# Emission order: products of generators that are due within a fixed time follow another generator's products at once

## The chip, the cores and the metric

One Trainium2 chip, one of its cores. The metric is the device time of one execution in microseconds (us), lower is better. The kernel before takes 3057.91 us (median of three runs, 3056.65 to 3059.26).

## What is computed

A two-layer backbone over 256 context and 256 latent tokens of width 2048. In each layer:

```python
xn  = rmsnorm(h) * (1 + scale) + shift           # shift, scale, gate = silu(c) @ ada_w + ada_b
u   = xn @ w_in                                  # one wide input projection
y_a = (groupnorm(wkv_scan(...)) + bonus) * silu(gate_a) @ w_out_a    # bidirectional RWKV-7, 16 heads of 64
y_b = (pool(u) @ pool_w) * silu(gate_b) @ w_out_b
h   = h + gate * ((mg0 * y_a + mg1 * y_b) @ w_out)                   # mg = sigmoid of columns of u
```

and a final rmsnorm of the latent half. The scan runs over 256 context tokens first and then over 256 latent tokens, in both directions.

## The kernel before, in words

All 512 tokens lie side by side in the free dimension; features lie on the 128 partitions. Weights stream from HBM in blocks of 512 KB into three buffers `wr`; each block is split on ScalarE into a high part `whi` and on VectorE into a low part `wlo`, and a projection of 128 outputs adds three products (high by high, high by low, low by high) for each of 16 slices of the input, 48 products of 512 (or, in layer 1, often 256) columns. These projections are the **main work**: a list of units, each of chunks and steps (`Main`, L366); one step is three products.

Beside it run **generators** (Python generators, L1371), in this order of precedence: `chain` (the scan over blocks of 64 tokens: tiles `ps_z`, `ps_a`, then `ps_y`, `ps_p`, `ps_y`), `gnorm` (`ps_c`, `ps_v`), `inv` (inverses of triangular blocks: `ps_M`, then `ps_Z` and `ps_W` in turn over six levels, `ps_R`, `ps_X`, `ps_T`, `ps_V`; one such generator in layer 0, two in layer 1), `prep` (`ps_kk`, `ps_d`, `ps_a`, `ps_b`, `ps_vr`) and `open_y`. A generator yields the time at which its next step is due. For a step with products that is `MG[l]` after its inputs are ready: 1000 ns in layer 0, 600 ns in layer 1.

The kernel is emitted in one pass with a clock for each engine (`E["pe"]`, `E["act"]`, ...; `clk`, L122), which are estimates in ns written into the kernel. `run` (L516) decides what comes next on all queues: if some generator's step is due (`t <= E["pe"]`), the first such one is emitted; otherwise `NS` = 2 steps of the main work (six products). Each engine executes its instructions in the order in which they were emitted.

The modulation vectors (`ada_blocks`, L559) are main work too. A block of `n` weight pieces adds its products into one tile `ps_ada`; after the last, `post` copies the sums to the one buffer `ada_r` (four small copies, ScalarE and VectorE in turn) and puts off the rest, `fin` (L595), to the time at which `ada_r` is expected: four products of `ada_r` with `comb` and some small VectorE operations. `flush_fins(n)` (L225) emits put-off `fin`s until no more than `n` are left. `step` calls `flush_fins(1)` (L466) before a unit's `pre`; `post` calls `flush_fins(0)` (L586) before it overwrites `ada_r`. Blocks of two pieces in succession stand in two places: in the first stretch of the kernel, interleaved with the units `ps_st`, and in the output projection of layer 0 (L1547), where each of the 16 units is a projection interleaved with one piece (`zipped`, L348): four steps of the projection (12 products), one of the piece, and so on, four times.

Of the kernel before, what the change touches and what calls it, by code (L numbers as in the profile page):

```python
# [8 lines left out]
R32 = mybir.dt.float32r  # L9
# [21 lines left out]
NU = (0, 1)  # L31
ZD = (0, 0)
N1, LA0, G0, LAG = 2, 20, 2, 4
AH, PACE, MG = 400.0, 600.0, (1000.0, 600.0)

V_MU, V_W0, V_A0, V_KK, V_KA, V_RK = 0, 24, 40, 56, 64, 80
# [10 lines left out]
def kernel(  # L47
# [65 lines left out]
    E = dict(pe=0.0, act=0.0, dve=0.0, pool=0.0, sp=0.0)  # L113
    rt, rd, old = {}, {}, {}

    def nm(ap):
        return ap.tensor.name

    def rdy(*aps):
        return max(rt.get(nm(a), 0.0) for a in aps)  # L120

    def clk(eng, cost, o, ins, lag=60.0):  # L122
        t = max(E[eng], rd.get(old.get(nm(o)), 0.0))
        for a in ins:
            t = max(t, rt.get(nm(a), 0.0))
        t += cost
        E[eng] = t
        rt[nm(o)] = t + lag
        for a in ins:
            rd[nm(a)] = t + lag  # L130
# [29 lines left out]
    def size(ap):  # L160
        n = 1
        for s in ap.shape[1:]:
            n *= s
        return n

    def mm(out, lhsT, rhs, start=True, stop=True, dep=True):
        nc.tensor.matmul(out=out, lhsT=lhsT, rhs=rhs, start=start, stop=stop)  # L167
        n, m = size(rhs), size(lhsT)
        dt = lhsT.dtype
        if dt == F32:  # L170
            c = 110 if m <= 32 else 360 if n < 32 else 1.6 * n if n > 64 else 190 if m > 64 else 78
        elif dt == R32:
            c = max(0.4225 * n, 109) + 75 * (kind[0] != dt)
        else:
            c = 28 if m > 64 else 18
        kind[0] = dt
        clk("pe", c, out, (lhsT, rhs) if dep else (), 200.0)

    kind = [R32]

    def act(out, in_, func=AF.Copy, scale=1.0, bias=None):
        kw = {} if bias is None else dict(bias=bias)
        nc.scalar.activation(out=out, in_=in_, func=func, scale=scale, **kw)  # L183
        c = (50 if psum(in_) else 90) + 0.84 * size(out) + 93 * ((not isinstance(scale, float)) + (bias is not None))
        clk("act", c, out, (in_,), 140.0)
# [4 lines left out]
    def tt(out, a, b, op, eng="dve"):  # L190
        ENG[eng].tensor_tensor(out=out, in0=a, in1=b, op=op)  # L191
        clk(eng, 65 + (1.05 if eng == "dve" else 2.0) * size(out), out, (a, b), 140.0)

    def stt(out, a, s, b, op0, op1):
        nc.vector.scalar_tensor_tensor(out=out, in0=a, scalar=s, in1=b, op0=op0, op1=op1)  # L195
        clk("dve", 65 + 1.05 * size(out), out, (a, b), 140.0)

    def ts(out, a, s1, op0, s2=None, op1=None, eng="dve"):
        kw = {} if op1 is None else dict(op1=op1)
        ENG[eng].tensor_scalar(out=out, in0=a, scalar1=s1, scalar2=s2, op0=op0, **kw)  # L200
        n = size(out)
        c = 75 + 1.8 * n if eng == "pool" else 120 + 0.95 * n if psum(a) else 60 + 0.52 * n if n > 300 else 75 + 0.65 * n
        clk(eng, c, out, (a,), 140.0)

    def cp(out, a, eng="dve"):
        ENG[eng].tensor_copy(out=out, in_=a)
        clk(eng, 50 + (0.7 if eng == "dve" else 3.8) * size(out), out, (a,), 140.0)
# [17 lines left out]
    def flush_fins(n):  # L225
        while len(fins) > n:
            late.remove(fins[0])
            fins[0][1]()

    def later(t, fn):  # L230

        x = (t, fn)
        late.append(x)
        return x

    def do_late(force=False):
        i = 0
        while i < len(late):
            if force or late[i][0] <= E["pe"]:
                late.pop(i)[1]()  # L240
            else:
                i += 1
# [239 lines left out]
    def pieces(src, load, ck, **kw):  # L482

        out = []
        for i in range(0, src.shape[1], load):
            g = dict(src=src[:, i:i + load], **kw)
            out += [dict(src=src[:, j:j + ck], grp=g, sl=slice(j - i, j - i + ck)) for j in range(i, i + load, ck)]
        return out
# [23 lines left out]
    def due(x):  # L512

        return max(x[0], piv.free("iv", x[1])) if isinstance(x, tuple) else x

    def run():  # L516

        while True:
            do_late()
            best, bt, held = None, None, True  # L520
            for g in gens:
                while g[1] is None:
                    g[1] = next(g[0], "end")
                    if g[1] is None:
                        break
                    held = False
                if g[1] == "end" or g[1] is None:
                    continue
                t = due(g[1])
                if best is None or t < bt:  # L530
                    best, bt = g, t
                if t <= E["pe"]:
                    best, bt = g, t
                    break
            gens[:] = [g for g in gens if g[1] != "end"]
            if best is None or bt > E["pe"]:
                mt = M.time()
                if mt is not None and (best is None or max(mt, E["pe"]) <= bt):
                    for _ in range(NS):
                        M.step()  # L540
                        do_late()
                        mt = M.time()
                        if mt is None or mt > E["pe"] + SL:
                            break
                    continue
            if best is None:
                if not gens and M.empty():
                    break
                if late:
                    do_late(True)  # L550
                elif held:
                    raise RuntimeError("stuck")
                continue
            E["pe"] = max(E["pe"], bt)
            best[1] = next(best[0], "end")
        do_late(True)


# [6 lines left out]
    def ada_block(l, b0, i, n, st, after, pre0, bank, slot):  # L565
        b = b0 + i
        nr = 2 * n

        def pre():
            if pre0:  # L570
                pre0()
            if i == 0:
                pl, tg = bank or (pmm, "mm")
                st["ps"] = pl.tile([128, T], F32, tag=tg, name="ps_ada")

        def mk(j):
            def step(c):
                for g in range(4):
                    mm(st["ps"][32 * g:32 * g + nr, 0:256], svp[:, 4 * j + g, 2 - 2 * i:2 - 2 * i + nr],
                       c["r"][:, g, :], start=i == 0 and j == 0, stop=i == n - 1 and j == 3)  # L580
            return (j, step)

        def post():
            if i < n - 1:
                return
            flush_fins(0)  # L586
            for g in range(4):
                q = slice(32 * g, 32 * g + nr)
                if g % 2:
                    cp(ada_r[q], st["ps"][q, 0:256])  # L590
                else:
                    act(ada_r[q], st["ps"][q, 0:256])
            fins.append(later(rdy(ada_r), fin))

        def fin():  # L595

            fins.pop(0)
            ps = st["ps"][:, 256:256 + 4 * n].rearrange("p (h i c) -> p h i c", h=2, c=2)
            for h in range(2):
                mm(ps[:, h].rearrange("p i c -> p (i c)"), ada_r[:, h * 128:(h + 1) * 128], comb[:, 0:2 * n])  # L600
            bias = lambda o, m: ve_t[:, l, o:o + m].unsqueeze(2).to_broadcast([128, m, 2])
            if b0 < KD:
                tt(modv[:, l, 0, b0:b0 + n, :], ps[:, 0], bias(V_AB + b0, n), ALU.add)
                m = modv[:, l, 1, b0:b0 + n, :]
                tt(m, ps[:, 1], bias(V_AB + 16 + b0, n), ALU.add)
                stt(m, m, 1.0, bias(V_NG + b0, n), ALU.add, ALU.mult)
            else:
                f = 2 * (b0 - KD)
                m = modv[:, l, 2, f:f + 2 * n, :]
                tt(m.rearrange("p (i h) c -> p h i c", h=2), ps,  # L610
                   bias(V_AB + 32 + f, 2 * n).rearrange("p (i h) c -> p h i c", h=2), ALU.add)
                ts(m, m, 0.5, ALU.mult)
            if after:
                for x in range(b0, b0 + n):
                    after(x)

        w = ada_w[l, b]
        if slot:
            ch = pieces(w, 8, 4, slot=slot)
        else:  # L620
            ch = pieces(w, 4, 4)
        return Unit(ch, [mk(j) for j in range(4)], pre, post, raw=True)


# [1062 lines left out]
```

## Time and profile before

| | before |
|---|---|
| median of three runs | 3057.91 us |
| the profiled execution | 3058.09 us |
| its span | 3056.3 us |
| TensorE busy (PE) | 2906.3 us, 95% |
| VectorE busy (DVE) | 1820.7 us, 60% |
| ScalarE busy (ACT) | 1457.3 us, 48% |
| GpSimd busy (POOL) | 149.7 us, 5% |
| mean granted TensorE clock | 0.978 |
| HBM | 139 GB/s over the span |

The span runs from the first to the last instruction. PE stands for matmul, PEld for the weight load that overlaps it, SP for the queue that issues DMAs. A matmul's end is modelled: successive matmuls overlap, so that the distance of their starts tells what one costs. By time the kernel falls into these stretches: until 160 us the first modulation vectors with the first projections (`ps_st`); 160 to 1381 us the projections of layer 0 with its generators; to 1597 us the two branch projections; to 1827 us the output projection of layer 0 with the modulation vectors of layer 1; to 1955 us the start of layer 1; to 2830 us its projections with its generators; then the rest.

### The profile page before, as it was taken

The numbers are of one execution on the slowest core, as the hardware profiler recorded it, in microseconds if no ns is written. First come the engines' busy times: TensorE is split into PE (matmuls) and PEld (weight loads), VectorE is DVE, ScalarE is ACT, GpSimd is POOL, SyncE is SP. The second block draws the span as 40 slices with busy tenths as digits, with TensorE's granted clock in tenths as the row PEclk, the third lists the DMA queues.
The fourth block names the chain that finished last, engine by engine and source line by source line (L and its number), as shares of the span: only waits on it lengthen the run. The fifth ranks groups of instructions, "written<-read, shape, count | busy, mean of one in ns | idle before, by whom it ended". The sixth has DMA issues, their size and how long they took to land.

```text
span 3056.3 us, 66262 instructions
## 1 busy us (share of the span) xinstructions
PE 2906.3 (95%) x27122; PEld 2292.5 (75%) x27122; DVE 1820.7 (60%) x4171; ACT 1457.3 (48%) x3092; POOL 149.7 (5%) x211
## 2 busy tenths in 40 slices
PE   5999999999999999998999989999999989999897
PEld 2687777767777777776876657887887768888797
DVE  3475666565655655534443235886786667775575
ACT  3254445445554554533222223666556646666454
POOL 2200000000000000000000002000000000000000
PEclk8999999999999999998999999999999989999899
DMA  9732222232333222327657764432333343344875
GB/s 361 256 121 72 78 76 91 72 116 94 112 111 118 87 80 87 94 88 248 205 190 225 234 222 124 141 117 85 108 94 111 119 127 99 111 122 129 260 251 161
DMA packets 158482, 427.74 MB, mean 140 GB/s; under 512 B 17376, under 2 KB 53600, under 8 KB 154080
## 3 DMA queue, kind: packets, MB, share of 16 engines
q1 hardware_dynamic: 133120, 390.32, 40.5%
q10 hardware_dynamic: 25056, 33.17, 3.0%
q8 instruction: 213, 3.49, 0.5%
q14 instruction: 93, 0.76, 0.1%
HBM read 389.21 MB, written 34.21 MB: 139 GB/s over the span
## 4 chain that ended last, share of the span: by engine, by line
PE 78%; DVE 8%; DMA 7%; ACT 5%; issue 2%; SPq 0%; POOL 0%; DVEq 0%; ACTq 0%; POOLq 0%
PE ps_mm L167 54%; PE ps_st L167 4%; DMA wr<-in_w_o 3%; DVE wlo L191 3%; PE ps_W L167 3%; PE ps_M L167 2%; PE ps_ada L167 2%; PE ps_y L167 2%; PE ps_a L167 2%; DMA wr<-in_w_in 2%; PE ps_Z L167 1%; PE ps_z L167 1%; PE ps_p L167 1%; ACT whi L183 1%; PE ps_T L1113 1%
## 5 line engine op out<-in xcount | busy, mean ns | idle before, releaser
L167 PE MATMUL ps_mm<-xh,whi 128*128 128x512 f32 (+1 forms) x2448 | 914.8, 374 | 8.2 <-ACT whi L183 3.1
L191 DVE TENSOR_TENSOR wlo<-wr,whi 128x512 fp32r<-128x512 f32 (+1 forms) x932 | 636.7, 696 | 444.8 <-ACT whi L183 439.1
L183 ACT ACTIVATE whi<-wr 128x512 fp32r<-128x512 f32 (+1 forms) x932 | 567.1, 619 | 671.3 <-PE ps_mm L167 336.7
L167 PE MATMUL ps_mm<-xh,wlo 128*128 128x512 f32 (+1 forms) x2448 | 855.2, 349 | 16.4 <-DVE wlo L191 15.7
L167 PE MATMUL ps_mm<-xl,whi 128*128 128x512 f32 (+1 forms) x2448 | 851.1, 348 | 0.0
L167 PEld LDWEIGHTS ps_mm<-xh,whi 128*128 128x128 f32 x2448 | 465.6, 190 | 91.9 <-issue 7.9
L167 PEld LDWEIGHTS ps_mm<-xh,wlo 128*128 128x128 f32 x2448 | 465.8, 190 | 83.5 <-DVE wlo L191 22.5
L167 PEld LDWEIGHTS ps_mm<-xl,whi 128*128 128x128 f32 x2448 | 467.6, 191 | 46.3 <-issue 1.0
L167 PE MATMUL ps_mm<-mgh,whi 128*128 128x512 f32 (+1 forms) x512 | 181.2, 354 | 2.9 <-ACT whi L183 2.9
L1024 DVE CAST_PREDICATED X<-pm_t,ps_W 128x128 f16<-128x128 uint8 x640 | 141.7, 288 | 65.2 <-PE ps_W L167 63.8
L167 PE MATMUL ps_mm<-mgh,wlo 128*128 128x512 f32 (+1 forms) x512 | 175.4, 343 | 0.0
L167 PE MATMUL ps_mm<-mgl,whi 128*128 128x512 f32 (+1 forms) x512 | 174.5, 341 | 0.0
L167 PE MATMUL ps_mm<-yh,whi 128*128 128x512 f32 (+1 forms) x512 | 129.0, 344 | 0.2 <-ACT whi L183 0.2
L167 PEld LDWEIGHTS ps_mm<-mgh,whi 128*128 128x128 f32 x512 | 98.2, 192 | 38.9 <-issue 19.3
L167 PE MATMUL ps_mm<-yl,whi 128*128 128x512 f32 (+1 forms) x512 | 125.4, 337 | 0.6 <-DVE m L195 0.5
L183 ACT ACTIVATE VS<-P 64x128 f32<-64x128 f32 x128 | 39.3, 307 | 167.3 <-DVE P L195 164.8
L183 ACT ACTIVATE zb<-ps_Z 128x512 f16<-128x512 f32 x144 | 85.2, 592 | 70.2 <-PE ps_Z L167 68.8
L167 PEld LDWEIGHTS <-X 64*64 64x64 f16 x2560 | 89.4, 110 | 35.7 <-issue 27.5
L191 POOL TENSOR_TENSOR nlo<-MM,n 64x512 f16<-64x512 f32 x48 | 62.8, 1308 | 1072.2 <-DVE X L1024 760.2
L167 PEld LDWEIGHTS ps_mm<-mgh,wlo 128*128 128x128 f32 x512 | 98.3, 192 | 14.5 <-DVE wlo L191 3.6
L167 PEld LDWEIGHTS ps_mm<-mgl,whi 128*128 128x128 f32 x512 | 98.4, 192 | 8.7
L167 PE MATMUL ps_ada<-wr,svp 128*4 128x256 f32 (+1 forms) x1024 | 83.2, 402 | 22.8 <-DMA wr<-in_ada_w 22.8
(258 smaller groups left out, 4353.2 us busy)
## 6 DMA issues: line engine op xcount, KB each, us to landing
wr<-in_w_in SPq DMA_DIRECT2D x306, 512.0 KB, 3.7
wr<-in_ada_w SPq DMA_DIRECT2D x128, 512.0 KB, 3.9
wbig<-in_ada_w SPq DMA_DIRECT2D x32, 1024.0 KB, 6.0
wr<-in_w_o SPq DMA_DIRECT2D x64, 512.0 KB, 4.8
wr<-in_w_b SPq DMA_DIRECT2D x32, 512.0 KB, 4.8
wr<-in_w_a SPq DMA_DIRECT2D x32, 512.0 KB, 4.0
wr<-in_w_st SPq DMA_DIRECT2D x32, 384.0 KB, 4.3
d_mg<-mth ACTq DMA_DIRECT2D x32, 256.0 KB, 2.0
```

Source lines behind the costliest of these rows:

```text
L167: nc.tensor.matmul(out=out, lhsT=lhsT, rhs=rhs, start=start, stop=stop)
L183: nc.scalar.activation(out=out, in_=in_, func=func, scale=scale, **kw)
L191: ENG[eng].tensor_tensor(out=out, in0=a, in1=b, op=op)
L1024: nc.vector.copy_predicated(dst.rearrange(pat, **kw)[:, :, :, u, :], m, src.rearrange(pat, **kw)[:, :, :, u, :])
L1113: nc.tensor.transpose(ps[:, j2, d, :], BK[:, d, c % 4].rearrange("p a t -> p (a t)"), ident)
```

## The change

Three edits. `run` counts the products of `mm` (`count`); when products were emitted since the main work's last steps (`count[0] != was`), a step counts as due if it is due up to `JOIN` = 600 ns after `E["pe"]`. A step with products that is taken so doesn't move `E["pe"]` to its due time; one without products does, and so does one that is due later still. And a block of modulation vectors emits all put-off `fin`s in its `pre`, before its own tile is taken, which comes before the unit's first step.

```diff
+JOIN = 600.0
 AH, PACE, MG = 400.0, 600.0, (1000.0, 600.0)
...
         kind[0] = dt
+        count[0] += 1
         clk("pe", c, out, (lhsT, rhs) if dep else (), 200.0)
 
-    kind = [R32]
+    kind, count = [R32], [0]
...
     def run():
 
+
+        was = -1
         while True:
             do_late()
+            now = E["pe"] + (JOIN if count[0] != was else 0)
             best, bt, held = None, None, True
...
-                if t <= E["pe"]:
+                if t <= now:
                     best, bt = g, t
                     break
             gens[:] = [g for g in gens if g[1] != "end"]
-            if best is None or bt > E["pe"]:
+            if best is None or bt > now:
                 mt = M.time()
...
                         if mt is None or mt > E["pe"] + SL:
                             break
+                    was = count[0]
                     continue
...
-            E["pe"] = max(E["pe"], bt)
+            n = count[0]
+            if bt > now:
+                E["pe"] = bt
             best[1] = next(best[0], "end")
+            if count[0] == n:
+                E["pe"] = max(E["pe"], bt)
         do_late(True)
...
             if pre0:
                 pre0()
             if i == 0:
+                flush_fins(0)
                 pl, tg = bank or (pmm, "mm")
                 st["ps"] = pl.tile([128, T], F32, tag=tg, name="ps_ada")
```

## Rows read from the trace of the kernel before

**Rows 1.** Windows, two long stretches: busy us (instructions) of each engine, granted clock, DMA
```profile
core 0: us, PE busy (x) PEld busy (x) DVE busy (x) ACT busy (x) POOL busy (x), PEclk, DMA share, GB/s
160.00:1381.00 1221.00, 1212.37 (x11295) 916.53 (x11297) 714.78 (x1665) 592.14 (x1258) 43.99 (x55) 1.00 0.30 94
1955.00:2830.00 875.00, 839.86 (x10570) 715.52 (x10573) 638.75 (x1640) 536.91 (x1228) 46.90 (x54) 0.98 0.37 112
```

**Rows 2.** Timeline of TensorE, output projection of layer 0: start, duration, what, idle before
```profile
1637.24 0.50 PE L167 MATMUL ps_mm<-mgh,whi 128*128 128x512 f32 x1
...
1639.88 0.39 PE L167 MATMUL ps_mm<-mgh,wlo 128*128 128x512 f32 x1
1641.59 0.61 PE L167 MATMUL ps_ada<-comb,ada_r 128*128 128x4 f32 x4 [1.33 <-DVE ada_r L206]
```

**Rows 3.** Waits of TensorE, 1400 to 1830 us: us in total, times, longest
```profile
PE ps_ada L167 <- DVE ada_r L206: 14.1, 8, 5.4
```

**Rows 4.** Chain that ended last, 1640 to 1657 us: start, us, what
```profile
1642.74 4.56 PE ps_mm L167 x12
...
1647.85 2.94 PE ps_mm L167 x12
...
1654.28 0.59 PE ps_ada L167 x8
...
1655.79 5.05 DMA wr<-in_w_o
```

**Rows 5.** Windows, just behind that wait
```profile
1641.60:1645.00 3.40, 3.40 (x19) 2.51 (x20) 0.78 (x3) 1.15 (x2) 0.00 (x0) 0.79 0.57 157
```

**Rows 6.** Chain that ended last, 59 to 66 us
```profile
59.47 0.59 PE ps_ada L167 x8
...
61.40 0.43 DVE ada_r L206
...
61.87 0.57 DVE wlo L191
...
62.48 1.89 PE ps_st L167 x7
```

**Rows 7.** Timeline of TensorE, layer 0: one step of `chain` alone, one of `inv` alone
```profile
1012.47 0.39 PE L167 MATMUL ps_mm<-xh,wlo 128*128 128x512 f32 x1
1012.79 0.45 PE L167 MATMUL ps_a<-Zs,X 64*64 64x64 f32 x8
...
1013.50 0.39 PE L167 MATMUL ps_mm<-xl,whi 128*128 128x512 f32 x1
...
1028.73 0.39 PE L167 MATMUL ps_mm<-xh,wlo 128*128 128x512 f32 x1
...
1030.01 0.39 PE L167 MATMUL ps_mm<-xl,whi 128*128 128x512 f32 x1
```

**Rows 8.** Timeline of TensorE, layer 1: the same two kinds in one group
```profile
2778.87 0.28 PE L167 MATMUL ps_mm<-xl,whi 128*128 128x256 f32 x1
2778.99 0.28 PE L167 MATMUL ps_mm<-xh,wlo 128*128 128x256 f32 x1
2779.20 0.45 PE L167 MATMUL ps_a<-Zs,X 64*64 64x64 f32 x8
2779.48 0.20 PE L167 MATMUL ps_W<-zbb,X 64*64 64x64 f16 x2
...
2780.30 0.28 PE L167 MATMUL ps_mm<-xl,whi 128*128 128x256 f32 x1
```

**Rows 9.** Timeline of TensorE: first products behind a group, with only six main products following
```profile
256.21 0.50 PE L167 MATMUL ps_mm<-xh,whi 128*128 128x512 f32 x1
...
1299.19 0.50 PE L167 MATMUL ps_mm<-xh,whi 128*128 128x512 f32 x1
...
1979.06 0.28 PE L167 MATMUL ps_mm<-xh,whi 128*128 128x256 f32 x1
...
2789.82 0.39 PE L167 MATMUL ps_mm<-xh,whi 128*128 128x256 f32 x1
```

**Rows 10.** Timeline of ScalarE: what the two steps of Rows 8 read
```profile
2777.49 0.26 ACT L183 ACTIVATE Zs<-ps_z 128x128 f32<-128x128 f32 x1
2777.85 0.60 ACT L183 ACTIVATE zbb<-ps_Z 128x512 f16<-128x512 f32 x1
```

**Rows 11.** Waits of TensorE, 1955 to 2830 us
```profile
PE ps_mm L167 <- DVE wlo L191: 12.3, 13, 2.2
```

## The prediction

> **What bounds the kernel now.** I read the windows first, stage by stage, because an average over 3 ms hides that the stages differ. In the two long stretches with generators TensorE is what ends the time: busy 1212 of 1221 us in layer 0, and 840 of 875 us in layer 1, where VectorE (639 us) comes next [rows 1]. So what changes there is worth its TensorE time, nearly one for one, and the generators' own latency is worth little. Then the chain that ended last, for the stretches with modulation vectors: in the output projection of layer 0 it goes through TensorE as well as through the DMAs of `w_o` and the four copies to `ada_r` [rows 2, 4], and in the first stretch through TensorE and these copies [rows 6]. Last, the timeline of TensorE alone, to see what a step of a generator costs alone and in company [rows 7, 8], and how often one follows another closely [rows 9].
>
> The profiled execution took 3058.09 us with a span of 3056.3 us; the median of the runs is 3057.91 us. The sum below is made against the span and carries over to the median unchanged, since they lie 0.01% apart beside a constant 1.8 us.
>
> **Part 1: `fin` at the head of the next block.** This is a small line with, I think, the most certain price. In the output projection a unit is: 12 products of the projection, one step of the modulation piece, and so on. When a block's second piece has ended, its sums are copied to `ada_r`, and these copies stand on ScalarE and VectorE behind the evacuation of the projection's own result. Now, the next unit's first 12 products run in that time, from 1637.24 to 1639.88 us, and only then `fin` waits, 1.33 us, until 1641.59 [rows 2]. With the change `fin` is emitted before these 12. TensorE takes its instructions in order, so behind the waiting `fin` all of them are queued: the wait begins at 1637.24 and lasts 1641.59 - 1637.24 = 4.35 us, and the 12 products come after it. What releases `ada_r` isn't sped up by this. So the block gets longer by the 12 products, that is 2.94 us at full clock [rows 4]. Whether that is on the path: behind `fin` the chain runs through four runs of main products and pieces to the piece that frees a buffer at 1654.28, and from there to the next DMA of `w_o` [rows 4], whose split precedes the next copies. No slack is seen between; so the delay repeats in each block. How many: all waits for `ada_r` in this stretch and the one before are 8, of 14.1 us [rows 3]; the longest, 5.4 us, ends a pair of pieces ahead of the branch projections and stays where it is. The other seven are blocks of this kind: 7 x 2.94 = +20.6 us. Nearest bounds: 0 if the DMA sets the block's length anyway (a rival, below), and 7 x 4.56 = 32 us if all these runs go at the clock that one of them shows. [...] A wait of 4.35 us can only make this more frequent; I add one more such run, 4.56 - 2.94 = 1.6. Part 1: **+22 us**, 0 to 32.
>
> In the first stretch the same line acts on six blocks. There the copies are on the chain already: after the piece ends at 60.06 (59.47 + 0.59), TensorE goes on with seven products of `ps_st` at 62.48, when a `wlo` queued on VectorE behind the last copy is done [rows 6]. With the change, `fin` starts when the last copy ends, 61.83 (61.40 + 0.43); the next piece's step and all nine `ps_st` come behind it instead of two of them before. The two cost 2 x 1.89/7 = 0.54 us; against them stands what is still left of the wait for `wlo`, 62.48 - 61.83 = 0.65, into which `fin` and the piece's step now fall. Between -0.1 and +0.5 us a block, the DMA doing the same; I take 0.2, so **+1 us**. The other pieces (single ones among the projections) have no `fin` pending when the next begins. Nothing is costed for them.
>
> **Part 2: the joined products.** A step of `chain` alone, `ps_a`, takes 1013.50 - 1012.47 = 1.03 us from the last main product before it to the second one behind; two distances of main products are in that, 0.24 each (2.64 us for 11 in [rows 2]), which leaves 0.55. A step of `ps_W` alone: 1030.01 - 1028.73 - 0.48 = 0.80 [rows 7]. Together in one group: 2780.30 - 2778.99 = 1.31, less two distances of 0.12 (256 columns), 1.07 [rows 8]. So putting one behind the other saves 0.55 + 0.80 - 1.07 = 0.28 us. What is saved is the change of kind at the group's ends: 128-square fp32 products to 64-square ones and back.
>
> [...]
>
> How many joins: I counted on TensorE's timeline the places where exactly two main steps (six products, at times five or seven records) stand between two generators' groups. In layer 0 there are 105, the first behind 256.21, the last behind 1299.19; in layer 1 147, of which 82 have 256 columns (from 1979.06 to 2789.82) [rows 9]. Behind these, the second step was not yet due at the end of the first and due one decision later. `JOIN` takes it if it was due within the first 0.6 us. Six main products of 512 columns cost the emission clock 6 x 0.216 + 0.075 = 1.37 us by L166, of 256 columns 0.73 us. If the due times lie evenly, 0.6/1.37 = 44% and 0.6/0.73 = 82% are joined: 46 in layer 0, 67 + 0.44 x 65 = 96 in layer 1. Each saves between 0 and 0.28; about half the pairs are of the kind that I could measure, so I take 0.15: 142 x 0.15 = **-21 us**, between -4 (a tenth of 0.28) and -40 (all).
>
> **Part 3: what the shorter margin costs.** The step joined in [rows 8] read `Zs`, ready at 2777.75, and `zbb`, ready at 2778.45 [rows 10]: 1.45 and 1.03 us before their products. A joined step loses the main pair that stood before it, 0.7 us with 256 columns, 1.4 us with 512. In layer 0 a margin of 400 to 1000 ns of the 1000 is left; in layer 1 0 to 600 of 600, with nothing for an error of the emission clock. Main products are queued behind a waiting product, so such a wait is lost in full. Bounds: 0, and the pair itself, about 0.7 us for a quarter of 96 steps, 17 us. I take 0.1 us for each of the 96: +10 us. Steps without products are joined also and stand earlier on VectorE, ahead of the splits for main work; TensorE waited 12.3 us for `wlo` in this stretch [rows 11], and half of that again, 6 us, is possible; it is left to the range. Part 3: **+10 us**, 0 to 23.
>
> **Sum.** 22 + 1 - 21 + 10 = +12: 3057.9 + 12 = 3070 us. The bulk of the gain is on the path, and so is the loss.
>
> **The rivals.** *Faster: the moved `fin` is hidden.* If in the output projection the DMAs set the length of a block, TensorE's 12 products are merely moved from before a wait to behind it, and the block stays. For it speaks that the chain goes through a `w_o` DMA of 5.05 us; it decides when TensorE has 2.94 us of slack between `fin` and the piece at 1654.28. Against it: no gap is printed in the rows between, and the DMA itself is issued behind that piece [rows 4]. Then 3070 - 22 = 3048 us; or, with a gain of 0.28 for each join, similar with half of Part 1. Chance 0.25. *Much slower: layer 1's margin.* Joined steps of layer 1 wait 0.3 us on the mean and `wlo` comes late: +30 instead of +10, 3090 us. For it: zero margin left at the limit; against: 1.0 us and more seen in [rows 10]. Chance 0.13. [...] Chance 0.1. *Nothing much:* few steps fall within 600 ns, and Part 1 is partly hidden, or the two cancel: within 6 us of before. Chance 0.1.
>
> **How the numbers follow.** The forecast, 3070 us (its own range 3060 to 3082), has 0.42. What a measurement of this kernel tells from no change is about 0.2%, 6 us. Slower: 0.42 + 0.13 + 0.1, less 0.03 for a forecast that falls short: 0.62. Same: 0.13. Faster: 0.25. The range takes in most of the faster rival and of the slow one: 3042 to 3092 us.
>
> **What would show it.** Part 1: in the output projection seven waits for `ada_r` of 4 to 5 us instead of 1.2 to 1.5, and the stretch longer by some 20 us. Part 2: fewer groups on TensorE in both layers, `ps_a` directly followed by `ps_W` more often, the stretches of [rows 1] shorter by 6 us and by 15 us before waits. Part 3: more waits of `ps_Z`, `ps_W`, `ps_a`, `ps_z` for ScalarE and VectorE in layer 1. I would be wrong in kind if the output projection keeps its length, and wrong in size if the joins number far more than 142.

## The result

The changed kernel takes 3126.28 us (median of four runs, 3121.22 to 3128.15), the kernel before beside it 3058.14 us: a ratio of 1.0226 [1.0214, 1.0238], 68 us slower. The forecast was 12 us slower, 3070, and its range ended at 3092. The profiled execution has a span of 3126.3 us, 70.0 more than before's.

For the comparison I cut both traces at the same places of the program: the *first stretch* runs from the first `ps_st` product of layer 0 to its first `ps_mm`, *layer 0* from there to the first `ps_ada` product behind its projections, the *output projection* from the first product of `mgh` to the first `ps_st` of layer 1, *layer 1* from its first `ps_mm` to the `ps_ada` behind its projections.

| us | before | after | difference | forecast |
|---|---|---|---|---|
| ahead of the first stretch | 44.5 | 50.7 | +6.2 | 0 |
| first stretch | 107.7 | 117.7 | +10.0 | +1 |
| layer 0 | 1228.5 | 1230.8 | +2.3 | -6.9 (46 joins) |
| output projection | 265.7 | 295.3 | +29.6 | +22 |
| layer 1 | 919.6 | 945.4 | +25.8 | -4.4 (96 joins, +10) |
| all the rest | 490.3 | 486.4 | -3.9 | 0 |

So no large part came out as forecast but the waits of the output projection. The windows tell busy time from idle; these are the four stretches of before (columns as in [rows 1], which are cuts of its second and fourth line):

```profile
44.50:152.20 107.70, 100.81 (x692) 65.09 (x693) 45.03 (x99) 30.13 (x63) 23.33 (x31) 0.98 0.77 284
152.20:1380.70 1228.50, 1219.87 (x11321) 922.83 (x11319) 720.80 (x1676) 596.79 (x1266) 43.99 (x55) 1.00 0.30 94
1577.10:1842.80 265.70, 243.25 (x1380) 154.13 (x1378) 79.57 (x160) 54.83 (x99) 1.36 (x2) 0.97 0.70 226
1909.60:2829.20 919.60, 882.15 (x10856) 755.13 (x10857) 677.34 (x1712) 566.65 (x1280) 47.01 (x55) 0.98 0.38 114
```

and of after, with one run of 12 products as a fifth line:

```profile
50.70:168.30 117.60, 108.22 (x692) 68.33 (x689) 41.00 (x90) 27.68 (x58) 18.07 (x29) 0.91 0.66 243
168.30:1399.10 1230.80, 1215.54 (x11321) 926.70 (x11319) 731.46 (x1684) 597.82 (x1269) 45.69 (x55) 1.00 0.30 95
1596.10:1891.40 295.30, 254.03 (x1380) 163.64 (x1378) 80.14 (x160) 54.82 (x99) 1.36 (x2) 0.91 0.64 202
1956.70:2902.10 945.40, 890.41 (x10858) 764.01 (x10856) 679.15 (x1722) 570.66 (x1288) 44.97 (x55) 0.97 0.36 111
1629.30:1636.00 6.70, 6.70 (x24) 4.76 (x24) 1.69 (x5) 1.15 (x2) 0.00 (x0) 0.53 0.39 125
```

The number of products is the same. In layer 0 TensorE is 4.3 us less busy (the joins) but 6.6 more idle. In layer 1 it is 8.3 us more busy and 17.5 more idle. In the output projection it is 18.8 us more idle, as forecast, and 10.8 more busy; in the first stretch 2.5 more idle and 7.4 more busy. More busy time with the same products is clock: the granted clock fell from 0.98 to 0.91 in the first stretch, from 0.97 to 0.91 in the output projection and from 0.98 to 0.97 in layer 1.

The timeline of TensorE in the output projection of after (start, duration, what, idle before) shows it at one block, in answer to [rows 2, 4]:

```profile
1624.41 0.61 PE L168 MATMUL ps_ada<-wr,svp 128*4 128x256 f32 x8
1629.30 1.02 PE L168 MATMUL ps_ada<-comb,ada_r 128*128 128x4 f32 x4 [4.28 <-DVE ada_r L208]
1630.18 0.78 PE L168 MATMUL ps_mm<-mgh,whi 128*128 128x512 f32 x1
1630.75 0.63 PE L168 MATMUL ps_mm<-mgl,whi 128*128 128x512 f32 x1
...
1635.57 0.61 PE L168 MATMUL ps_ada<-wr,svp 128*4 128x256 f32 x8
```

`fin` waits 4.28 us, and the 12 products that used to fill this time stand behind it. From the first of them to the next piece they take 5.39 us instead of 2.94: a product each 0.43 us instead of 0.23, with a granted clock of 0.53 (the last window above). Behind all seven waits these runs of 12 take 4.30 to 5.40 us, 34.5 us together, where 2.94 each would be 20.6. The waits for `ada_r` in this stretch are now seven, none under 4.1 us:

```profile
PE ps_ada L168 <- DVE ada_r L208: 30.9, 7, 4.7
```

In before the same seven made up 14.1 - 5.4 = 8.7 us of [rows 3]. In the first stretch each of five blocks has a wait for `ada_r` that wasn't there, in answer to [rows 6]:

```profile
64.72 0.61 PE L168 MATMUL ps_ada<-wbig,svp 128*4 128x256 f32 x8
67.21 0.61 PE L168 MATMUL ps_ada<-comb,ada_r 128*128 128x4 f32 x4 [1.88 <-DVE ada_r L208]
67.75 0.61 PE L168 MATMUL ps_ada<-wbig,svp 128*4 128x256 f32 x8
68.29 0.50 PE L168 MATMUL ps_st<-xh,whi 128*128 128x512 f32 x1
68.63 0.46 PE L168 MATMUL ps_st<-xl,whi 128*128 128x512 f32 x1
68.89 0.63 PE L168 MATMUL ps_st<-xh,wlo 128*128 128x512 f32 x1
...
72.01 1.13 PE L168 MATMUL ps_ada<-wbig,svp 128*4 128x256 f32 x16
```

and from the third on at the latest, the `ps_st` behind it go at 0.43 us each. Before, each of these blocks had another wait, of 1.37 us for `wlo`, between products of 512 columns; behind that one the clock stayed up. Here are the waits of the stretch (after, then before), one wait of before, and the window behind one wait of after and of before:

```profile
PE ps_ada L168 <- DVE ada_r L208: 9.4, 5, 1.9
PE ps_st L167 <- DVE wlo L191: 6.8, 5, 1.4
62.48 0.50 PE L167 MATMUL ps_st<-xh,wlo 128*128 128x512 f32 x1 [1.37 <-DVE wlo L191]
68.90:72.00 3.10, 3.10 (x8) 1.97 (x6) 1.28 (x2) 1.05 (x2) 1.45 (x3) 0.50 0.31 130
62.48:64.20 1.72, 1.72 (x7) 1.43 (x8) 0.41 (x1) 0.10 (x1) 0.00 (x0) 1.00 1.06 435
```

Ahead of this stretch two such `fin`s wait, 1.88 and 6.04 us:

```profile
PE ps_ada L168 <- DVE ada_r L208: 7.9, 2, 6.0
```

The first `ps_st` starts at 50.7 us instead of 44.5; in all runs below it starts at 44.2 to 46.5 us without the moved line and at 49.0 to 50.5 with it.

For layer 1, the waits of TensorE (columns as in [rows 11]) of after, and as a fifth line the one for `wlo` of before between the same two places:

```profile
PE ps_T L1124 <- DVE X L1035: 9.5, 3, 4.2
PE ps_mm L168 <- DVE wlo L193: 6.5, 12, 1.9
PE ps_ada L168 <- DVE ada_r L208: 4.6, 4, 2.4
PE ps_M L168 <- DVE MM L193: 4.1, 10, 0.8
PE ps_mm L167 <- DVE wlo L191: 14.4, 15, 2.2
```

The waits for `wlo`, which I feared, fell; what grew most are waits of generators' own products, for `X` (2.3 us in before) and `MM`.

### The profile page after: what moved, and what is told of

It is laid out like the page before. It is cut to its first block, busy times and chain, and to the rows that moved or that the text cites. A ratio compares the mean times of both kernels' runs of the same rounds, so it can differ in the third digit from the quotient of the medians.

```text
span 3126.3 us, 66257 instructions
## 1 busy us (share of the span) xinstructions
PE 2926.6 (94%) x27122; PEld 2315.7 (74%) x27122; DVE 1824.6 (58%) x4171; ACT 1455.5 (47%) x3092; POOL 147.2 (5%) x211
## 5 line engine op out<-in xcount | busy, mean ns | idle before, releaser
L168 PEld LDWEIGHTS ps_mm<-mgh,whi 128*128 128x128 f32 x512 | 100.8, 197 | 34.5 <-issue 21.7
L168 PEld LDWEIGHTS ps_mm<-mgh,wlo 128*128 128x128 f32 x512 | 100.5, 196 | 12.6 <-DVE wlo L193 0.6
```

## Experiments

Times in us; the ratio is to the kernel before run beside it (3052.77 to 3055.26 us), the stretches are those of the profiled execution. The expectations of `flush_only` and `join_products` count layer 1 from a later place, where it has 907 us in before and 932 in after.

| run | median | ratio | first | layer 0 | output | layer 1 |
|---|---|---|---|---|---|---|
| flush_only | 3097.60 | 1.0141 [1.0101, 1.0182] | 117.5 | 1228.2 | 293.3 | 918.5 |
| join_only | 3082.36 | 1.0098 [1.0075, 1.0121] | 107.8 | 1235.1 | 261.8 | 942.3 |
| join_l0 | 3056.76 | 1.0004 [0.9993, 1.0016] | 107.0 | 1230.1 | 264.3 | 922.4 |
| join_products | 3051.02 | 0.9989 [0.9978, 1.0001] | 107.8 | 1224.5 | 261.3 | 919.9 |
| join_noclock | 3043.65 | 0.9960 [0.9944, 0.9975] | 106.9 | 1230.1 | 265.4 | 903.9 |
| flush_warm | 3144.40 | 1.0290 [1.0269, 1.0310] | 124.1 | 1233.8 | 325.7 | 920.8 |
| flush_warm2 | 3073.05 | 1.0061 [1.0045, 1.0078] | 110.4 | 1228.4 | 277.9 | 915.8 |
| shift_before | 3053.61 | 0.9993 [0.9982, 1.0004] | 108.1 | 1228.5 | 259.1 | 917.9 |
| shift_join | 3077.21 | 1.0073 [1.0056, 1.0090] | 107.7 | 1231.2 | 261.8 | 940.7 |
| before_mg580 | 3053.04 | 0.9992 [0.9978, 1.0007] | 107.8 | 1228.6 | 264.2 | 919.8 |
| join_mg580 | 3070.66 | 1.0054 [1.0036, 1.0072] | 108.2 | 1234.5 | 262.4 | 929.5 |
| before_mg620 | 3064.39 | 1.0030 [1.0016, 1.0045] | 107.9 | 1228.1 | 264.3 | 927.1 |
| join_mg620 | 3080.04 | 1.0095 [1.0065, 1.0124] | 107.5 | 1232.5 | 260.6 | 940.1 |
| products_mg620 | 3048.48 | 0.9977 [0.9965, 0.9989] | 106.4 | 1224.3 | 265.9 | 913.1 |
| noclock_mg620 | 3051.86 | 0.9995 [0.9983, 1.0007] | 107.7 | 1229.6 | 267.4 | 911.7 |
| late_fin | 3031.57 | 0.9925 [0.9908, 0.9941] | 106.9 | 1227.3 | 251.3 | 907.0 |
| products_late | 3009.01 | 0.9849 [0.9834, 0.9863] | 107.5 | 1217.6 | 252.0 | 898.4 |
| noclock_late | 3032.14 | 0.9929 [0.9912, 0.9946] | 107.0 | 1223.6 | 249.4 | 916.4 |

### The two edits apart

`join_only` is the changed kernel without the line in `pre`; `flush_only` is the kernel before with that line alone.

```diff
             if i == 0:
-                flush_fins(0)
                 pl, tg = bank or (pmm, "mm")
```

> The changed kernel without the call of flush_fins(0) in the block's pre; the joining stays. By landmarks of the two traces the changed kernel lost 16 us up to the end of the first stretch, 2 us in layer 0, 29 us in the output projection and 25 us in layer 1. If the two edits are independent, this run keeps only the losses of the two long stretches: 3058 + 27 = 3085 us, with the first stretch ending near 137 us and the output projection back at 247 us. If the early fins also disturb what the generators do later, layer 1 comes back too and the run is at 3060 us or below.

> The kernel before with the call of flush_fins(0) in the block's pre alone. Independent edits: 3058 + 16 + 29 = 3103 us, with waits of 1.9 us for ada_r in the first stretch and of 4 to 5 us in the output projection, layer 1 unchanged at 907 us. My prediction's own terms for this line were 22 + 1, 3081 us. If the DMAs set the output projection's length: below 3070 us.

The two cost 28 and 43 us, 72 together, where the whole change cost 68. The stretches separate cleanly: the moved `fin` has all of the first stretch and the output projection, the joins all of layer 1. So there are two questions.

### Why the moved `fin` costs twice what the waits explain

The theory is that the lower clock behind each wait costs, beside the wait. To test it, constant products are put into the unused half of the new tile ahead of the `fin`; they fill the wait and delay nothing if they are few enough.

```diff
                 st["ps"] = pl.tile([128, T], F32, tag=tg, name="ps_ada")
+                if fins and not pre0:
+                    for _ in range(WARM[bank is not None]):
+                        nc.tensor.matmul(out=st["ps"][0:4, 288:480], lhsT=svp[:, 0, 0:4], rhs=cs_t[:, 0:192], ...)
+                flush_fins(0)
```

> As flush_only (3098 us), but the new tile is taken first and TensorE computes constants into its unused half ahead of the early fins: 16 products in the first stretch, 34 in the output projection, some 0.1 us each, in the time in which it would wait for ada_r. They add work that nobody needs. Theory: a part of the loss is the clock: the first stretch showed 21 us at the lower level in flush_only against 5 before, the output projection 55 us against 18. If so the first stretch comes back from 117.5 to about 110 us and the output projection from 293 to about 277, the run to 3070 to 3078 us. Rival: the wait alone is the loss; then nothing changes, 3095 to 3105 us.

`flush_warm` had 16 and 34 of them. One took 0.335 us, not some 0.1, so they lasted longer than the waits (5.36 us for 1.88), and the run says nothing on the price. `flush_warm2` has 5 and 12:

> The moved fin alone (3097.6 us), with constant products on TensorE ahead of it, now sized by what one took, 0.335 us: 5 in the first stretch for a wait of 1.88 us and 12 in the output projection for waits of 4.2 to 4.7 us. If the lower clock that follows the waits is what makes the first stretch 117.5 us instead of 107.7, it goes back to 110 to 113 us, with at most 8 us at the lower clock instead of 21; and the output projection goes from 293 to 280 to 288 us. If the wait itself costs it, the first stretch stays at 117 us or more. Total 3080 to 3090 or 3095 to 3100 us.

The timeline of TensorE in its first stretch, at the same block as above:

```profile
64.82 0.61 PE L168 MATMUL ps_ada<-wbig,svp 128*4 128x256 f32 x8
65.25 1.79 PE L578 MATMUL ps_ada<-cs_t,svp 128*4 128x192 f32 x10
67.31 0.61 PE L168 MATMUL ps_ada<-comb,ada_r 128*128 128x4 f32 x4 [0.27 <-DVE ada_r L207]
...
70.69 1.05 PE L168 MATMUL ps_ada<-wbig,svp 128*4 128x256 f32 x16
```

`fin` starts as late as in after, 2.49 us behind the piece before it, but from `fin` to the next piece it is 3.38 us instead of 4.80 (72.01 - 67.21). In the output projection, too, the way from the piece before to `fin` is as long as without these products (31.1 us in the seven blocks together, 31.5 in `flush_only`), but the 12 products behind it take 2.90 to 2.94 us in each block, instead of 4.44 to 5.40. The windows of the first stretch and the output projection, `flush_only` first:

```profile
49.00:166.50 117.50, 108.13 (x693) 69.12 (x690) 41.00 (x90) 27.72 (x59) 18.07 (x29) 0.91 0.66 244
1592.80:1886.20 293.40, 254.49 (x1380) 163.28 (x1378) 80.19 (x160) 54.80 (x99) 1.36 (x2) 0.91 0.63 204
```

then `flush_warm2`:

```profile
50.50:160.90 110.40, 109.06 (x742) 67.88 (x739) 41.01 (x90) 27.66 (x59) 18.09 (x29) 0.98 0.71 259
1586.00:1864.00 278.00, 266.05 (x1548) 166.12 (x1546) 79.83 (x160) 54.81 (x99) 1.36 (x2) 0.98 0.67 215
```

With more work to do, TensorE is through 7.1 and 15.4 us earlier, at a clock of 0.98 instead of 0.91, and the kernel gains 24.5 us of the 43, more than I expected (3080 to 3090 us). `fin` starts as late as before; so more than half of the price of the moved line is the clock behind its waits. That is shown.

### Why the joins cost in layer 1

Two theories: the shorter margin of joined products (Part 3), or the steps without products, which the window takes early too. `join_l0` joins in layer 0 alone. `join_products` joins only steps with products; the others come when they came before.

```diff
-            now = E["pe"] + (JOIN if count[0] != was else 0)
+            near = JOIN if count[0] != was else 0
+            now = E["pe"]
...
                 t = due(g[1])
+                if t > now and t <= now + near and prod(g[1]):
+                    t = now
```

> No early fins, and the window of 600 ns in layer 0 alone (0 in layer 1). If the margin theory holds (layer 0 has 1000 ns of margin, so 400 to 1000 are left): layer 0 gains what is saved at the groups' ends, 6 us by my prediction, and loses few waits: 3052 to 3060 us. If joining itself costs (whatever the margin), about 3060 and above, as the 2 us of the changed kernel.

> No early fins, joining in both layers, but of steps with products alone: steps without products stay due as before and never move the clock forward. Theory A, the shorter margin of products costs layer 1: it stays at 925 to 932 us, the run at 3078 to 3085 us. Theory B, the steps without products that are taken early (they move the emission clock forward and stand on VectorE and ScalarE ahead of the splits) cost it: layer 1 at 907 us or below, the run at 3035 to 3060 us.

In layer 0 the joins alone, without flushing, cost 1.6 and 6.6 us (`join_l0` and `join_only`, which have the same order there); the 6 us that `join_l0` was to gain there didn't come. Joining only steps with products gains 4.0 us there and costs nothing in layer 1 (919.9), although nearly as many groups were joined: with the modulation pieces counted as main work, 250 groups of generators' products stand between main work in layer 1 (310 in before, 237 in after). So not the margin of products: the steps without products. Their windows (layer 1, then layer 0), `join_only` first:

```profile
1912.60:2854.90 942.30, 888.11 (x10862) 762.49 (x10864) 678.78 (x1722) 570.39 (x1288) 45.01 (x55) 0.97 0.37 111
152.00:1387.10 1235.10, 1217.98 (x11324) 927.79 (x11324) 733.32 (x1684) 597.30 (x1269) 44.55 (x55) 1.00 0.30 94
```

then `join_products`:

```profile
1902.30:2822.10 919.80, 878.29 (x10857) 753.86 (x10856) 676.48 (x1720) 569.95 (x1287) 46.89 (x55) 0.98 0.37 113
152.00:1376.40 1224.40, 1213.88 (x11321) 925.27 (x11319) 731.09 (x1684) 598.41 (x1269) 44.80 (x55) 1.00 0.30 95
```

They can cost in two ways: by their place on VectorE and ScalarE, or because each sets `E["pe"]` to its due time, up to 600 ns ahead, while TensorE has done nothing for it. `join_noclock` takes them by the same window as the change does, but leaves the clock alone (two polls of a generator that would then come without end are kept out of the window).

```diff
-            n = count[0]
             if bt > now:
                 E["pe"] = bt
             best[1] = next(best[0], "end")
-            if count[0] == n:
-                E["pe"] = max(E["pe"], bt)
```

> Joining of all steps, no early fins (as join_only, 3082 us with 942 us in layer 1), but a step without products that is taken early no longer moves the emission clock to its due time (the two places where a generator merely asks again later are left out of the window, else it would never move). Clock theory: the loss comes from the clock running ahead, so that main products are missing between a generator's steps: layer 1 returns to 920 us, the run to 3050 to 3060 us. Queue theory: it comes from where these steps stand on VectorE and ScalarE, which is as early as in join_only or earlier: layer 1 stays at 940 us or more, the run at 3080 us or more.

```profile
1912.10:2816.00 903.90, 868.33 (x10790) 746.95 (x10789) 672.10 (x1707) 567.20 (x1274) 47.09 (x55) 0.99 0.38 116
152.40:1382.50 1230.10, 1216.22 (x11321) 926.94 (x11319) 731.73 (x1684) 599.41 (x1269) 44.60 (x55) 1.00 0.30 95
```

Layer 1 falls to 903.9 us, 16 us below what the clock theory expected, and the kernel becomes faster than before. TensorE is idle for 35.6 us instead of 54.2, and busy for 868.3 instead of 888.1, with a granted clock of 0.99 instead of 0.97. The waits for `X` (9.5 us, the longest 4.2, in `join_only` as in after) are not among its longest any more. So in layer 1 the loss hangs on the moved clock. What it brings with it isn't parted from it: with the moved clock the window reaches further, so that more steps without products fall into it (75 in layer 1 of `join_only`, 47 here, as the two programs are emitted), and the two polls are in it.

In layer 0 the unmoved clock brings nothing back. It has 1230.1 us there, 5.7 more than `join_products`, and a second pair of executions of these two orders (`noclock_mg620`, `products_mg620`) says the same, 1229.6 and 1224.3. So there it is the early steps without products themselves that cost.

### Is that the rule, or one order?

Any change of a due time gives another order for the whole of layer 1, and orders differ by themselves. First I set the emission clock 500 ns ahead once, at the start of layer 1, in the kernel before and in `join_only`.

> The kernel before, with the emission clock of TensorE set 500 ns ahead once, at the start of layer 1, and nothing else. It asks how much the projections of layer 1 (919.6 us before) vary when the same rules meet another phase of the clock. If a difference in this stretch stands for a rule: 915 to 925 us here, total within 6 us of before. If the order in layer 1 depends on the phase so much that single stretches can't be compared: 905 us or less, or 935 us or more.

> The joining edit alone, with the same 500 ns at the start of layer 1. If steps without products that are taken early and move the clock are what costs, the projections of layer 1 stay near the 942.3 us of the joining alone: 935 to 950 us, total 3075 to 3090. If the 942.3 us are an accident of the phase: 915 to 930 us, total 3055 to 3070.

This moved all later due times alike, so the order stayed as it was: the runs are repetitions. `flush_only`, `flush_warm`, `flush_warm2` and `join_l0` have the order of before in layer 1 as well, instruction for instruction on TensorE, VectorE and ScalarE. These six executions of one order take 915.8 to 922.4 us, and three of the order with all joins (after, `join_only`, `shift_join`) 940.7 to 945.4. The output projection in the order of before takes 259.1 to 267.4 us in the 13 runs that have it. Then I changed the margin of layer 1 from 600 to 580 and 620 ns, which does give other orders.

```diff
-AH, PACE, MG = 400.0, 600.0, (1000.0, 600.0)
+AH, PACE, MG = 400.0, 600.0, (1000.0, 620.0)
```

> The kernel before with a margin of 620 ns instead of 600 in layer 1. It gives another order by the same rules. If the rules set the projections of layer 1: 912 to 928 us (919.6 before). If single orders scatter more than the rules differ: outside 905 to 935 us.

> Joining of all steps, with a margin of 620 ns in layer 1. If the moved emission clock is what costs: 935 to 950 us for the projections of layer 1 (942.3 with 600 ns). If 942 was an accident of the order: 925 us or less.

> Joining only of steps with products, with a margin of 620 ns in layer 1. By the rule: 912 to 928 us for the projections of layer 1 (919.9 with 600 ns), at least 15 us under the joining of all steps. If orders scatter: anything between 900 and 945.

> Joining of all steps where those without products, taken early, don't move the emission clock, with a margin of 620 ns in layer 1. By the rule: 900 to 922 us for the projections of layer 1 (903.9 with 600 ns, 916.4 with the later fin). If the steps without products cost by their place on VectorE and ScalarE and the 903.9 was an accident: 935 us or more.

> The kernel before with a margin of 580 ns instead of 600 in layer 1. By the rule: 912 to 928 us for the projections of layer 1. If single orders scatter more than the rules differ: outside 905 to 935 us.

> Joining of all steps, with a margin of 580 ns in layer 1. By the rule: 935 to 950 us for the projections of layer 1, some 22 us over the kernel before with the same margin. If 942 was an accident of the order: within 10 us of it.

Layer 1 with 580, 600 and 620 ns: before 919.8, 919.6, 927.1; all joins 929.5, 942.3, 940.1. Joining costs 9.7, 22.7 and 13.0 us, 15 on the mean. With 580 ns my expectation failed: 9.7 us is not the 22 of the rule but just within the 10 that were to stand for an accident of the order. The medians of these pairs are 17.6, 28.2 and 15.7 us apart. The two margins of the other rules (600 and 620 ns): only products 919.9 and 913.1; clock not moved 903.9 and 911.7, which is 15.7 and 15.4 us *less* than before with the same margin. Orders of one rule differ by 7 to 13 us, repetitions of one order by up to 6.6. The sign of joining all steps stands in each pair; of the 23 to 26 us of after, some 8 to 11 are this order's own.

### The opposite of the moved `fin`

If waits for `ada_r` cost clock, a `fin` put off further should gain. `late_fin` is the kernel before with 3000 ns more (outside the first stretch), `products_late` is `join_products` with it, `noclock_late` is `join_noclock` with it.

```diff
-            fins.append(later(rdy(ada_r), fin))
+            fins.append(later(rdy(ada_r) + (0 if after else 3000), fin))
```

> The kernel before, with fins put off 3000 ns more on the emission clock, except in the first stretch: the opposite of the early fins. Seven waits of 1.2 to 1.5 us for ada_r in the output projection and three runs at the lower clock behind them should go, and up to 5 us of such waits among the projections: 3058 - 9 - 5 = 3040 to 3050 us. If the DMAs set the output projection's length: 3055 us and above.

> join_products with the late fins of late_fin. If both gains are what they seem (3 and about 12 us) and independent, 3038 to 3046 us, faster than both kernels of this case.

> Joining in which steps without products that are taken early don't move the emission clock (3043.65 us alone), together with the fin put off by 3000 ns more (3031.57 us alone, 23.7 less than before). If the two gains are of different places they add: 3020 us. If the later fin gains more once steps are joined, as in the version that joins only steps with products (3009 us): 3000 to 3012 us. If both gain by the same idle time of TensorE: 3030 us.

`late_fin` gains more than expected, 24 us (3040 to 3050 us was the forecast). Its waits of TensorE in the output projection:

```profile
PE ps_ada L167 <- DMA wr<-in_ada_w: 6.8, 3, 3.2
PE ps_mm L167 <- ACT whi L183: 3.2, 5, 1.4
PE ps_nrm L167 <- DVE acc L191: 2.0, 1, 2.0
```

The waits for `ada_r` are gone, and the stretch has 251.3 us: 8 to 16 less than in the 13 executions of before's order (259.1 to 267.4). The other 12.6 us are in layer 1, where few `fin`s stand. Its order is another one there (321 groups instead of 310), and the gain is more than before's repetitions and other orders scatter. TensorE is 6.0 us less busy and 6.6 less idle; why this order does better I didn't find. With `products_late`, 3009.01 us, ratio 0.9849 [0.9834, 0.9863], there is a version that beats both kernels: layer 0 1217.6 and layer 1 898.4 us. It gains 46 us, where its two edits alone gain 3 and 24 and I expected 3038 to 3046; in layer 1 the granted clock is 1.00. Layer 1 of `late_fin`, then of `products_late`:

```profile
1894.10:2801.10 907.00, 876.17 (x10857) 751.45 (x10857) 672.18 (x1712) 566.44 (x1280) 48.85 (x55) 0.99 0.38 116
1883.70:2782.10 898.40, 864.68 (x10858) 744.33 (x10856) 675.64 (x1720) 571.18 (x1287) 46.11 (x55) 1.00 0.38 116
```

`noclock_late` doesn't add its two gains (3020 us would have been that): layer 1 has 916.4 us, 12.5 more than without the later `fin` and 9.4 more than `late_fin`, which joins nothing. So that the unmoved clock gains 15 us in layer 1 holds for two margins and not for each order.

## Why the prediction was wrong

**Part 1, output projection: the wait was right, the clock behind it mis-sized.** The wait that begins at the next block's head and lasts 4.35 us came true: 4.17 to 4.75 us, seven times, and 18.8 us more idle time against 7 x 2.94 = 20.6. The step that failed is "I add one more such run, 4.56 - 2.94 = 1.6". The row for it was there, 4.56 us and a clock of 0.79 after a wait of 1.33 us [rows 4, 5]; I wrote that a longer wait makes it more frequent and then priced one run. That it does was my estimate, without a row; the traces bear it out: such runs of 12 took 4.30 to 4.56 us behind three of the seven waits in before, and longer than 2.94 us behind all seven in after. With all seven at 4.30 to 5.40 us it is 10.8 us more busy time in the trace, and filling the waits gave back 15.4. The 7 x 4.56 = 32 us that I named as a bound was nearly the price, 29.6.

**Part 1, first stretch: both terms missed.** I had "between -0.1 and +0.5 us a block", from a `fin` that starts when the last copy ends. So it does, and the exchange of waits that I compared is small: 1.88 us for `ada_r` instead of 1.37 for `wlo`, 2.5 us more idle in the whole stretch. The step that failed is that I priced idle time alone, although the new wait stands elsewhere: behind it the nine `ps_st` run almost all at half the clock (0.50 granted from 68.90 to 72.00 us), behind the old one they didn't (1.00). That is 7.4 us of busy time. And the blocks ahead of the first stretch, where a `fin` waits 6.04 us, I had not looked at: +6.2 us.

The traces show the clock behind these waits: products follow each other at 0.43 us instead of 0.23, and where products on constants fill the waits the clock of both stretches is 0.98 instead of 0.91. By what rule the clock falls they don't show. The length of the wait alone doesn't tell: in the output projection of before waits of 1.33, 1.48 and 1.50 us were followed by 12 products in 4.56, 4.55 and 4.30 us, one of 1.38 us by 12 in 2.94.

**Part 2, the joins: number nearly right, gain smaller, and lost again in layer 0.** Places with six main products between groups (modulation pieces counted as main work) fell from 100 to 59 in layer 0 (46 joins forecast) and from 146 to 44 in layer 1 (96 forecast); all groups became fewer by 43 and 73. The 0.28 us of a pair came true as well. This is one in layer 0 of after, in answer to [rows 7, 8]:

```profile
437.93 0.40 PE L168 MATMUL ps_mm<-xh,wlo 128*128 128x512 f32 x1
438.26 0.45 PE L168 MATMUL ps_a<-Zs,X 64*64 64x64 f32 x8
438.54 0.20 PE L168 MATMUL ps_W<-zb,X 64*64 64x64 f16 x2
...
439.48 0.40 PE L168 MATMUL ps_mm<-xl,whi 128*128 128x512 f32 x1
```

439.48 - 437.93 less two distances of 0.24 is 1.07 us, against 0.55 + 0.80 alone. On the mean of all joins it is less: 4.3 us of busy time over 46 joins is 0.09 each, where I took 0.15; the six executions of this order of layer 0 give 1.9 to 5.3 us, 0.04 to 0.11 each. What the prediction had at nothing is the idle time that goes with it: 6.6 us more in layer 0, where `join_products` has 1.9 more and `join_noclock` 5.3. No run shows the 0.15 itself: it was an estimate, 0.28 for about half of the pairs, and no run here parts the kinds of pairs. What the trace does show by kind are the ends of a group. In layer 0 of before the way from a main product to the next start, where nothing waits, is 0.32 us on the median if `ps_a` or `ps_W` follows (64*64 in the rows) and 0.23 if `ps_Z` follows (128*128) or another main product; the first main product behind `ps_a` or `ps_W` takes 0.34 us to the second, behind `ps_Z` 0.31.

**Part 3: the wrong mechanism.** Of the 58 us between forecast and measurement 30 stand in layer 1, more than in any other stretch. I priced a margin of products, 0.1 us for each of 96 joins. `join_products` keeps that short margin and has layer 1 as before, 919.9 us. The cost sits with the steps without products, and in layer 1 in a line that I had described and not followed: a step without products moves `E["pe"]` to its due time. I had such steps in mind only as earlier instructions on VectorE, "ahead of the splits", and left 6 us to the range; the waits for `wlo` fell instead. What the moved clock does is to let the emission believe that TensorE is up to 600 ns further than it is. My reading, which fits the waits for `X` and `MM` but has no run of its own, is that products are then emitted before their inputs are there, with the main work that could have filled the time behind them. That the moved clock, with the further reach that it gives the window, costs in layer 1 is shown: 38 and 28 us between all joins and the unmoved clock at two margins. With 600 ns, 18.6 of the 38 are idle time and 19.8 busy time, part of it the granted clock again (0.97 against 0.99).

**The rivals.** "The moved `fin` is hidden" fell: the output projection grew by 29.6 us. "Much slower: layer 1's margin" had the place and a price nearer to the measured one (+30 instead of +10), by a mechanism that `join_products` refutes. The sign was the one that I held likeliest, at 0.62. The range was short: even my own upper bounds together (32 for the output projection, 6 x 0.5 for the first stretch, -4 and 23 for the joins) give 3112 us, because what stood ahead of the first stretch, the clock in it and the moved clock in layer 1 had no term at all.

## What to carry to other kernels

Price a new wait on TensorE twice: its own length, and, where rows show the granted clock to fall behind such waits, the products behind it at the clock of those rows (here down to 0.50, a product each 0.43 us instead of 0.23), for each occurrence. Where an emission order is made with an estimated clock, be wary of taking steps early that give the engine of that clock no work, above all when they move the clock: what that shifts is everything judged by the clock afterwards. The version that left such steps as they were lost nothing in either layer. Before a few microseconds are credited to a rule of ordering, try the rule on two or three orders: here one order of the same rule differed from the next by 7 to 13 us, and one order from its own repetition by up to 6.6.

## What I had not expected of the hardware

A wait of 1.88 us between products of `ps_ada` was followed, in five blocks of five, by a granted clock of 0.56 or 0.57 over the nine `ps_st` behind it, while a wait of 1.37 us between products of 512 columns left the clock at 1.00 (62.48 to 64.20 us of before). With five products of no use in the longer wait the `ps_st` behind it went at 0.23 us each (68.97 to 70.37 us of `flush_warm2`), and the clock of the first stretch was 0.98 instead of 0.91: with twelve more in each wait of the output projection, the kernel with the useless products (3073.05 us) is 24.5 us faster than the one without (3097.60).
